# Two tiny activations moved, and the planner's costs corrected, in a one-core mixer layer

## The chip, the cores and the metric

The kernel runs on one core of a Trainium2 chip. The core has five engines with queues of their own: TensorE (PE) multiplies matrices into PSUM, VectorE (DVE) and ScalarE (ACT) work on elements, GpSimd (POOL) does the same more slowly and issues transfers that add to what lies at their target, and SyncE (SP) issues the plain transfers. Each engine runs its queue strictly in order, so an instruction that waits holds up everything behind it on that engine. ScalarE computes functions from tables; a function whose table is not the one in use needs an ACT_TABLE_LOAD in front of it.

The metric is the device time of one execution in microseconds, as the median over runs. A profiled execution gives the trace.

## The reference

One layer on x of 1024 tokens by 1024 channels, all in float32:

```python
c_act = jax.nn.silu(c)
mod = c_act @ mod_w[l] + mod_b[l]
shift, scale, gate = jnp.split(mod, 3, axis=-1)
h = rmsnorm(x, norm_g[l]) * (1.0 + scale[:, None, :]) + shift[:, None, :]
u = h @ w_in[l]                                   # 1024 -> 5 x 1024
cv, cg, cs, lx, ls = jnp.split(u, [...], axis=-1)

v = causal_depthwise_conv(cv * sigmoid(cg), dw_w[l], dw_b[l])      # 31 taps
v = silu(layernorm(v, cln_g[l], cln_b[l]))
y_conv = (v @ pw2_w[l] + pw2_b[l]) * silu(cs)

xs = causal_depthwise_conv(lx, sc_w[l], sc_b[l])                   # 4 taps
r, i = sigmoid(xs @ wr + br), sigmoid(xs @ wi + bi)                # 8 heads
log_a = -8 * r * softplus(-lam[l])
a = exp(log_a); mult = sqrt(-expm1(2 * log_a))
hs = linear_scan(a, mult * (i * xs))
y_lru = hs * silu(ls)

y = concatenate([y_conv, y_lru]) @ w_out[l]
out = rmsnorm(x + (1.0 + gate) * y, final_g)
```

## The kernel before

**Layout.** Channels lie on the 128 partitions, in KT = 8 tiles, and the 1024 tokens along the free axis, in two halves of 512. Every float32 operand of a large product is split into two parts, hi (rounded to the type that TensorE multiplies) and lo (the remainder), and a product is three matmuls: hi·hi, hi·lo and lo·hi. The hi of a weight is a cast on ScalarE (`whi`); its lo (`wlo`) comes by one of three ways, by the weight's number in the order: a subtraction on GpSimd (below EARLY = 20), a subtraction on VectorE (below LATE = 41), or a transfer. In the last way, `remainder` (L470), ScalarE writes the negated hi into `wlo` and GpSimd issues a transfer that adds the weight from HBM (for `ylc`, a tile) to it (`ADD`, L385). These transfers are the "DMA remainders": seven for the recurrent half of w_out (`wlo<-in_w_out_dram`), and some for the point-wise and last products (`wlopw`, `hlpw`, `wloout`, `hlout`, `ylc`).

**Stages.** (1) The start, to about 57 us: c goes through Silu and is spread over the partitions by TensorE, eight dot products on VectorE with mod_w give the scale, x is scaled into `uh` and `ul`, and the first four column tiles of w_in are multiplied (`first0` to `first3`, in PSUM). The RMS norm's divisor is only known once all of x has been squared: TensorE sums the squares (`token_stats`), ScalarE takes the root (L939, tile `st`), VectorE the reciprocal, and TensorE spreads it over the partitions, one half of the tokens at a time, from where ScalarE copies it to `rbc`. VectorE then multiplies the finished products by `rbc` (`first_u`). The second half of the fourth product has no PSUM buffer until then; it is computed afterwards, under the name `late`. (2) To about 472 us: the other 36 column tiles of w_in, eight pairs of gate products, with the convolutions, scans and the rest of the dot products on the other engines. (3) To about 565 us: the recurrent half of w_out, eight products of 48 matmuls (`ps<-yh,whi` and so on), and beside them the layer norm of the convolution: mean by TensorE, subtraction on VectorE and squares on ScalarE tile by tile (`lnss`, `lnsq`), sums by TensorE, root on ScalarE (`sd`), reciprocal, spread (`lnbc`), multiplication on VectorE, Silu on ScalarE. (4) To about 633 us the point-wise product (`xpw`, `ypw`, `zpw`), and (5) to the end the convolution's half of w_out (`xout`, `yout`, `zout`, `y`) with the final norm; both by a scheme of seven half-sized products in place of eight.

**How the order comes about.** Nothing in the program runs in the order in which it is written. Every operation is handed to a planner (class `Plan`) with an engine, a cost in microseconds, a priority (lower is sooner), and what it reads and writes. `Plan.order` plays a clock forward and, on each engine that is free, takes the ready operation with the lowest priority that finds its buffers free; the instructions are then emitted in the order of this play. So the planner's costs decide the order on the chip but not the time there. The costs that matter here:

- `SWITCH` (L131): what an activation costs more in the plan if its function's table is not in use. When choosing, 2.0 is added to the priority of such an operation. Abs, Square, copies and scalings have no table of their own in the plan.
- `LAND` (L93): how long after its issue a DMA remainder counts as landed, at the least.
- 0.18 us for each of the small matmuls that sum a block of 128 tokens (L727 in `rstd`, and L983).
- `LATENCY`: what passes until another engine, or the same, may use a result; 0.15 for ScalarE and VectorE.

An operation's result is not due before these times, and ScalarE, when it has nothing else that is ready, takes whatever is, whatever its priority.

**What the change touches.** The root of a constant at L753: an activation with Sqrt of one column, into `junk`, whose only use is that its table load stands early. `softplus8` (L1009): softplus of lam for eight values a partition, from Abs and Exp on ScalarE (tile `sp_u`) and a row of tiny VectorE operations. `layer_norm` (L1235). A second root of a constant stands ahead of the last product (L1441) and stays.

Of the kernel before, what the change touches and what calls it, by code (L numbers as in the profile page):

```python
# [11 lines left out]
AF = mybir.ActivationFunctionType  # L12
# [5 lines left out]
KT = D // P  # L18
# [71 lines left out]
GDOT = "DVE"  # L90
FOLD = "DVE"
EARLY = 20
LATE, LAND = 41, 4.5  # L93
ISSUE, FLIGHT, RATE = 1.0, 10.0, 3.0
GM = 17
TAPP = 25
# [29 lines left out]
class Plan:  # L126
# [1 line left out]


    LATENCY = {"SP": 2.0, "PE": 0.2, "ACT": 0.15, "DVE": 0.15, "POOL": 0.15}  # L130
    SWITCH = 1.3  # L131
    TICK, BUSY, COLD = 3.4133, 3060, 3.8

    def __init__(self, pools):
# [176 lines left out]
def hymba_layer(ctx: ExitStack, tc: tile.TileContext, xT, vecs, mod_w, w_first, w_in,  # L311
# [37 lines left out]
    def ACT(prio, out, in_, func, n=T, bias=None, scale=None, accum=None, r=(), w=(),  # L349
            reserve=0, after=()):  # L350
        kw = {}

        def emit():
            if func == "copy":
                act.copy(out(), in_())  # L355
                return
            if bias is not None:
                kw["bias"] = bias
            if scale is not None:
                kw["scale"] = scale  # L360
            if accum is not None:
                kw["accum_out"] = accum
            act.activation(out=out(), in_=in_(), func=func, **kw)  # L363
        ptr = sum(x is not None and not isinstance(x, float) for x in (bias, scale))
        return S.op("ACT", a_cost(n, ptr) + (0.1 if accum is not None else 0), emit, prio, r, w,
                    table=SETS.get(func), reserve=reserve, after=after)
# [48 lines left out]
    def halves(b, a, e):  # L415
        return [(b, i) for i in range(b.parts) if i * (T // b.parts) < e
                and a < (i + 1) * (T // b.parts)]
# [287 lines left out]
    def rstd(prio, sqs, a, e, ps, o, after=(), warm=(), idle=None):  # L705


        nb = (e - a) // P
        sd, rs = S.buf("sd", f"sd{prio}_{o}"), S.buf("rs", f"rs{prio}_{o}")
        wk = halves(ps, o, o + e - a)  # L710


        def warm_mm():
            pe.matmul(half(idle, 0)()[:, :P], ones, ones, start=True, stop=True)

        def stats(sq, k):
            for b in range(nb):
                pe.matmul(ps()[:, o + b:o + b + 1], sq()[:, a + b * P:a + b * P + P],
                          ones[:, 0:1], start=k == 0 and b == 0, stop=k == len(sqs) - 1,
                          skip_group_check=True)  # L720

        def spread(ps=ps):
            for b in range(nb):
                pe.matmul(ps()[:, o + b * P:o + b * P + P],
                          rs()[:, b:b + 1].to_broadcast([P, P]), ident, start=True, stop=True)
        for k, sq in enumerate(sqs):
            at = S.op("PE", 0.18 * nb, lambda sq=sq, k=k: stats(sq, k), prio, halves(sq, a, e), wk,  # L727
                      after=after if k == 0 else [])
            for _ in range(warm[k] if warm else 0):
                S.op("PE", 0.22, warm_mm, prio, [], [idle], after=[at], columns=4 * P)  # L730
        ACT(prio, lambda: sd()[:, :nb], lambda: ps()[:, o:o + nb], AF.Sqrt, nb, bias=eps_t,
            scale=1.0 / D, r=wk, w=[sd])
        S.op("DVE", 0.2, lambda: dve.reciprocal(rs()[:, :nb], sd()[:, :nb]), prio, [sd], [rs])
        op = S.op("PE", 0.22 * nb, spread, prio, [rs], wk, columns=4 * P * nb)
        if idle:
            S.op("PE", 0.22 * nb, lambda: spread(idle), prio, [rs], [idle], after=[op],
                 columns=4 * P * nb)
        return wk, op
# [11 lines left out]

    cs, ps_c = ctile("cs", KT), [mm_tile(f"c_row{z}") for z in (0, 1)]
    ACT(-130, lambda: cs, lambda: V[:, OFF["c"]:OFF["c"] + KT], AF.Silu, KT, w=[("cs", 0)])
    ACT(-101, lambda: junk, lambda: eps_t, AF.Sqrt, 1, r=[("cs", 0)], w=[("junk", 0)])  # L753

    def idle_mm():
        pe.matmul(psb()[:, :P], ones, ones, start=True, stop=True)
# [222 lines left out]
    def shift_mm():  # L979
        for i in range(len(FIRST + NEXT)):  # L980
            pe.matmul(psx()[:, i:i + 1], fsum()[:, i * P:i * P + P], ones[:, 0:1],
                      start=True, stop=True)
    S.op("PE", 0.18 * len(FIRST + NEXT), shift_mm, BIP, [fsum], [psx])  # L983
    ACT(BIP, lambda: bias, lambda: psx()[:, :len(FIRST + NEXT)], "copy", len(FIRST + NEXT), r=[psx],
        w=[("bias", 0)])

# [21 lines left out]

    def softplus8(pr, after):  # L1009
        lam = lambda: V[:, OFF["lam"]:OFF["lam"] + KT]  # L1010
        u, s, s2, q, r = (S.buf("sp_" + n, "sp_" + n) for n in ("u", "s", "s2", "q", "r"))
        ACT(pr, u, lam, AF.Abs, KT, w=[u])
        ACT(pr, u, u, AF.Exp, KT, scale=-1.0, r=[u], w=[u])
        TS(pr, s, u, 2.0, None, ALU.add, r=[u], w=[s], after=after)
        S.op("DVE", 0.2, lambda: dve.reciprocal(s(), s()), pr, [s], [s])
        TT(pr, "DVE", s, s, u, ALU.mult, KT, r=[s, u], w=[s])
        TT(pr, "DVE", s2, s, s, ALU.mult, KT, r=[s], w=[s2])
        TS(pr, q, s2, 1.0 / 17.0, 1.0 / 15.0, ALU.mult, ALU.add, r=[s2], w=[q])
        for n in (13, 11, 9, 7, 5, 3, 1):
            TT(pr, "DVE", q, q, s2, ALU.mult, KT, r=[q, s2], w=[q])  # L1020
            TS(pr, q, q, 1.0 / n, None, ALU.add, r=[q], w=[q])
        TT(pr, "DVE", q, q, s, ALU.mult, KT, r=[q, s], w=[q])
        TS(pr, r, lam, -1.0, 0.0, ALU.mult, ALU.max, w=[r])
        STT(pr, q, q, 2.0, r, ALU.mult, ALU.add, KT, r=[q, r], w=[q])
        TS(pr, lambda: sp8n, q, -8.0, None, ALU.mult, r=[q], w=[("sp8", 0)])
        TS(pr, lambda: sp8h, q, 4.0, None, ALU.mult, r=[q], w=[("sp8", 1)])
# [208 lines left out]
    def layer_norm():  # L1235
        pr = 45
        mean, hi, lo = mm_tile("mean"), big_buf("csh", F32R), big_buf("csl", F32R)
        split(-1, hi, lo, csum)
        for rhs, last in ((hi, False), (lo, True)):
            def mean_mm(rhs=rhs, last=last):  # L1240
                for a, b in FULL:
                    pe.matmul(mean()[:, a:b], ones_d, rhs()[:, a:b], start=not last, stop=last)
            S.op("PE", 2 * 0.2267, mean_mm, -1, [rhs], [mean], columns=2 * H)
        ss = big_buf("lnss")
        for t in range(KT):
            TT(pr, "DVE", c[t], c[t], mean, ALU.subtract, r=[c[t], mean], w=[c[t]])
            if t == 0:
                ACT(pr, ss, c[t], AF.Square, r=[c[t]], w=[ss])
            else:
                q = big_buf(f"lnsq{t}")  # L1250
                ACT(pr, q, c[t], AF.Square, r=[c[t]], w=[q])
                TT(pr, "DVE", ss, ss, q, ALU.add, r=[ss, q], w=[ss])
        bc = mm_tile("lnbc")
        rstd(-1, [ss], 0, T, bc, 0)
        for t in range(KT):
            TT(pr, "DVE", c[t], c[t], bc, ALU.mult, r=[c[t], bc], w=[c[t]])
            ACT(pr, c[t], c[t], AF.Silu, scale=vec("cln_g", t), bias=vec("cln_b", t), r=[c[t]],
                w=[c[t]])
# [266 lines left out]
```

## Time and profile before

| | |
|---|---|
| median of 3 runs | 733.63 us (732.92 to 734.35) |
| profiled execution | 734.38 us, of which the span from first to last instruction is 732.5 us |
| granted TensorE clock | 0.996 |
| TensorE / VectorE / ScalarE / GpSimd busy | 99% / 83% / 63% / 22% of the span |
| table loads on ScalarE | 45, 1.283 us each, 57.7 us in all |
| DMA remainders for the recurrent half | 7, 512 KB each, 6.3 to 9.8 us from the start of the issue to the landing |

A row of the order of time reads: start in us, length in us, engine, line, operation, what it writes <- what it reads, shapes, count, and in brackets the engine's idle time just before it and what ended it. Rows that follow one another on an engine may be merged into one with a count. A row of the list of waits reads: who waited, <- for whom, us in total, times, longest. A matmul's row is longer than the distance from one matmul's start to the next, since they overlap: 512 columns start every 0.227 us.

### The profile page before, as it was taken

How to read it: one execution, taken by the hardware profiler on the slowest of the kernel's cores; microseconds unless marked ns; L12 is line 12 of the kernel's file. 1: busy time of each engine (PE TensorE's matmuls, PEld its weight loads, DVE VectorE, ACT ScalarE, POOL GpSimd, SP SyncE). 2: the span in 40 equal slices, each digit the busy share in tenths (PEclk: the TensorE clock that was granted, in tenths of full speed). 3: DMA queues.
4: the chain of work that ended last, by engine and by line, in shares of the span. 5: the costliest groups of instructions: out<-in, count | busy, mean ns of one | idle time of the engine just before them, and what ended most of it. 6: DMA issues, size and time to landing. Idle time of an engine off the chain costs nothing.

```text
span 732.5 us, 8976 instructions
## 1 busy us (share of the span) xinstructions
PE 722.9 (99%) x3292; PEld 601.2 (82%) x3292; DVE 611.2 (83%) x832; ACT 459.4 (63%) x579; POOL 159.6 (22%) x147
## 2 busy tenths in 40 slices
PE   9999999999999999999999999999999999999996
PEld 8888888888888887888888888888888888878885
DVE  7999999989559996888598999839698566999647
ACT  7650677656669759956848789517594345755322
POOL 0024012344524222232215111320000001010003
PEclk9999999999999999999999999999999999999998
DMA  8961023358888999799753644686666846784006
GB/s 342 408 223 58 0 82 84 86 115 191 196 209 183 239 243 215 179 224 211 161 114 85 154 90 120 173 233 174 170 158 152 227 117 138 221 217 167 20 15 216
DMA packets 40508, 121.03 MB, mean 165 GB/s; under 512 B 4496, under 2 KB 13200, under 8 KB 40464
## 3 DMA queue, kind: packets, MB, share of 16 engines
q0 software_dynamic: 15552, 43.70, 33.0%
q1 hardware_dynamic: 23904, 75.84, 30.3%
q10 hardware_dynamic: 1008, 0.92, 0.4%
q8 instruction: 26, 0.43, 0.2%
q14 instruction: 18, 0.15, 0.1%
HBM read 72.55 MB, written 12.58 MB: 116 GB/s over the span
## 4 chain that ended last, share of the span: by engine, by line
PE 69%; DVE 13%; issue 11%; DMA 3%; ACT 3%; POOL 1%; DVEq 0%; POOLq 0%; ACTq 0%
PE ps L506 46%; PE xout L675 5%; PE xpw L675 5%; PE ypw L675 3%; DVE modw L374 2%; DVE caccs L374 2%; PE gate L1205 2%; PE y L650 2%; PE zpw L675 1%; DMA wloout<-in_w_out_dram 1%; DVE ul L374 1%; DVE cacc L374 1%; PE zout L675 1%; DMA oo<-co 1%; DMA wlo<-in_w_out_dram 1%
## 5 line engine op out<-in xcount | busy, mean ns | idle before, releaser
L506 PE MATMUL ps<-uh,whi 128*128 128x512 f32 x576 | 177.6, 390 | 0.3 <-ACT scs L363 0.3
L506 PE MATMUL ps<-ul,whi 128*128 128x512 f32 x576 | 177.4, 389 | 0.0
L506 PE MATMUL ps<-uh,wlo 128*128 128x512 f32 x576 | 177.3, 389 | 0.0
L506 PEld LDWEIGHTS ps<-uh,whi 128*128 128x128 f32 x576 | 107.9, 188 | 23.3 <-ACT scs L363 1.0
L506 PEld LDWEIGHTS ps<-ul,whi 128*128 128x128 f32 x576 | 108.1, 188 | 22.5
L506 PEld LDWEIGHTS ps<-uh,wlo 128*128 128x128 f32 x576 | 108.1, 188 | 22.5
L355 ACT CAST whi<-raw 128x1024 fp32r<-128x1024 f32 x44 | 45.9, 1047 | 69.9 <-PE ps L506 44.9
L387 POOL DMA_DIRECT2D es<-cq x45 | 41.1, 936 | 128.0 <-ACT cq L363 91.7
L382 POOL TENSOR_TENSOR wlo<-raw,whi 128x1024 fp32r<-128x1024 f32 x16 | 40.3, 2530 | 126.0 <-ACT whi L355 85.1
L363 ACT ACT_TABLE_LOAD x45 | 57.7, 1283 | 5.8 <-DMA oo<-co 4.3
L374 DVE SCALAR_TENSOR_TENSOR cacc<-v,V,cacc 128x511 f32<-128x511 f32 (+14 forms) x75 | 55.6, 742 | 0.5
L374 DVE SCALAR_TENSOR_TENSOR caccs<-v,V,caccs 128x511 f32<-128x511 f32 (+6 forms) x70 | 52.1, 744 | 2.3 <-ACT caccs L363 1.1
L374 DVE SCALAR_TENSOR_TENSOR caccs<-c,wsum,caccs 128x511 f32<-128x511 f32 (+6 forms) x70 | 52.0, 743 | 1.0
L387 POOL DMA_DIRECT2D oo<-co x42 | 37.9, 948 | 61.7 <-ACT co L363 25.3
L506 PE MATMUL ps<-yh,wlo 128*128 128x512 f32 x128 | 39.6, 391 | 0.2 <-DMA wlo<-in_w_out_dram 0.2
L506 PE MATMUL ps<-yh,whi 128*128 128x512 f32 x128 | 39.6, 391 | 0.0
L506 PE MATMUL ps<-yl,whi 128*128 128x512 f32 x128 | 39.5, 389 | 0.0
L382 DVE TENSOR_TENSOR wlo<-raw,whi 128x1024 fp32r<-128x1024 f32 x21 | 27.5, 1311 | 5.8 <-ACT whi L355 5.8
L363 ACT ACTIVATE cq<-v,V 128x511 f32<-128x511 f32 (+14 forms) x45 | 31.8, 706 | 0.1
L374 DVE SCALAR_TENSOR_TENSOR xs<-ps,V,xs 128x1023 f32<-128x1023 f32 (+2 forms) x24 | 30.6, 1273 | 0.0
L374 DVE SCALAR_TENSOR_TENSOR modw<-modw,sc 128x1024 f32<-128x1024 f32 x23 | 30.1, 1312 | 0.0
L363 ACT ACTIVATE cq<-c,wsum 128x512 f32<-128x512 f32 x42 | 29.6, 711 | 0.0
(334 smaller groups left out, 1458.1 us busy)
## 6 DMA issues: line engine op xcount, KB each, us to landing
raw<-in_w_in_dram SPq DMA_DIRECT2D x36, 512.0 KB, 4.5
modw<-in_mod_w_dram SPq DMA_DIRECT2D x24, 512.0 KB, 7.9
scsd<-scs SPq DMA_DIRECT2D x8, 512.0 KB, 4.3
raw<-in_w_out_dram SPq DMA_DIRECT2D x8, 512.0 KB, 4.1
accd<-acc SPq DMA_DIRECT2D x8, 512.0 KB, 4.5
rawpw<-in_pw_dram SPq DMA_DIRECT2D x8, 512.0 KB, 4.1
scsr<-scsd SPq DMA_DIRECT2D x8, 512.0 KB, 4.9
rawout<-in_w_out_dram SPq DMA_DIRECT2D x8, 512.0 KB, 3.3
```

What stands on the lines that cost most here:

```text
L355: act.copy(out(), in_())
L363: act.activation(out=out(), in_=in_(), func=func, **kw)
L374: dve.scalar_tensor_tensor(out=out(), in0=in0(), scalar=scalar, in1=in1(), op0=op0, op1=op1, accum_out=accum)
L382: lambda: e.tensor_tensor(out=out(), in0=a(), in1=b(), op=op), prio, r, w,
L387: return S.op("POOL", ISSUE, lambda: pool.dma_start(out(), a(), accum_op=ALU.add), prio, r, w, lag=RATE * n / T, after=after, flight=flight)
L506: pe.matmul(ps()[:, a - off:b - off], k3(lhs)()[:, k, :], rhs[k]()[:, a:b], start=(k == 0 and lhs is wh and rhs is xh and (a - off) % H == 0),
L650: pe.matmul(to(), half(*lhs)()[:, j * P:j * P + P], half(*rhs)()[:, c0:c1], start=a == "S1" and j == 0 and t == 0, stop=j == KT // 2 - 1 a ...
L675: pe.matmul(half(ps, 0)(), half(*lhs)()[:, j * P:j * P + P], half(*rhs)(), start=start and j == 0 and t == 0, stop=j == KT // 2 - 1 and t ...
L1205: pe.matmul(ps()[:, c0:c1], lhs()[:, j, :], rhs()[:, c0:c1], start=st == 0, stop=st == 2)
```

## The change

The Abs and Exp of `softplus8` leave that function and are given priorities −129 and −128, straight after the Silu of c; the root of a constant now waits for Exp's result and has priority −127 (before: −101, after the Silu of c). In the layer norm, another root of the constant is put after the first square, with priority −1. The planner's numbers become LAND 6.0, SWITCH 1.283 and 0.224 for the small sums.

```diff
-LATE, LAND = 41, 4.5
+LATE, LAND = 41, 6.0
...
-    SWITCH = 1.3
+    SWITCH = 1.283
...
-            at = S.op("PE", 0.18 * nb, lambda sq=sq, k=k: stats(sq, k), prio, halves(sq, a, e), wk,
+            at = S.op("PE", 0.224 * nb, lambda sq=sq, k=k: stats(sq, k), prio, halves(sq, a, e), wk,
...
     ACT(-130, lambda: cs, lambda: V[:, OFF["c"]:OFF["c"] + KT], AF.Silu, KT, w=[("cs", 0)])
-    ACT(-101, lambda: junk, lambda: eps_t, AF.Sqrt, 1, r=[("cs", 0)], w=[("junk", 0)])
+    sp_u = S.buf("sp_u", "sp_u")
+    ACT(-129, sp_u, lambda: V[:, OFF["lam"]:OFF["lam"] + KT], AF.Abs, KT, w=[sp_u])
+    ACT(-128, sp_u, sp_u, AF.Exp, KT, scale=-1.0, r=[sp_u, ("cs", 0)], w=[sp_u])
+    ACT(-127, lambda: junk, lambda: eps_t, AF.Sqrt, 1, r=[sp_u], w=[("junk", 0)])
...
-    S.op("PE", 0.18 * len(FIRST + NEXT), shift_mm, BIP, [fsum], [psx])
+    S.op("PE", 0.224 * len(FIRST + NEXT), shift_mm, BIP, [fsum], [psx])
...
-        u, s, s2, q, r = (S.buf("sp_" + n, "sp_" + n) for n in ("u", "s", "s2", "q", "r"))
-        ACT(pr, u, lam, AF.Abs, KT, w=[u])
-        ACT(pr, u, u, AF.Exp, KT, scale=-1.0, r=[u], w=[u])
+        u = sp_u
+        s, s2, q, r = (S.buf("sp_" + n, "sp_" + n) for n in ("s", "s2", "q", "r"))
...
-                ACT(pr, ss, c[t], AF.Square, r=[c[t]], w=[ss])
+                o = ACT(pr, ss, c[t], AF.Square, r=[c[t]], w=[ss])
+                ACT(-1, lambda: junk, lambda: eps_t, AF.Sqrt, 1, w=[("junk", 0)], after=[o])
```

## The prediction

> **What bounds the kernel now.** I read the busy shares first, then TensorE's own list of waits, then the order of time at the places where that list has an entry, because only there can a change shorten the run.
>
> ```profile
> PE 722.9 (99%) x3292; PEld 601.2 (82%) x3292; DVE 611.2 (83%) x832; ACT 459.4 (63%) x579; POOL 159.6 (22%) x147
> ...
> PE token_stats L756 <- DVE ones L432: 1.1, 1, 1.1
> PE finbc L724 <- DVE rs65.7_0_5731 L733: 0.9, 1, 0.9
> PE late L799 <- DVE first_u L382: 0.8, 1, 0.8
> PE xout L675 <- DMA wloout<-in_w_out_dram: 0.4, 1, 0.4
> PE ps L506 <- ACT scs L363: 0.3, 1, 0.3
> PE ps L506 <- DMA wlo<-in_w_out_dram: 0.2, 1, 0.2
> ```
>
> TensorE works through 99% of the span, and the change gives it the same 3292 matmuls. All its waits together are 3.7 us: 1.1 at the very start, 0.9 in the closing norm, and four in between of 0.8, 0.4, 0.3 and 0.2. So the gain has a floor: what the change does to ScalarE counts only as far as it reaches one of these waits or makes a new one.
>
> **The start: exponential before root.** ScalarE's first 6 us, and the place where the first root is needed for the result:
>
> ```profile
> 3.05 1.28 ACT L363 ACT_TABLE_LOAD   x1
> 4.34 0.20 ACT L363 ACTIVATE junk<-eps_t 128x1 f32<-128x1 f32 x1
> 4.57 1.28 ACT L363 ACT_TABLE_LOAD   x1
> 5.86 0.21 ACT L363 ACTIVATE sp_u<-sp_u 128x8 f32<-128x8 f32 x1
> 5.97 0.57 ACT L355 COPY sc<-c_row 128x512 f32<-128x512 f32 x1
> ...
> 43.20 1.28 ACT L363 ACT_TABLE_LOAD   x1
> 43.43 1.22 DVE L374 SCALAR_TENSOR_TENSOR modw<-modw,sc 128x1024 f32<-128x1024 f32 x1
> 44.50 0.27 ACT L363 ACTIVATE st<-token_stats,eps_t 128x8 f32<-128x8 f32 x1
> 46.56 1.05 PE L934 MATMUL token_stats<-ident,st 128*128 128x128 f32 x8
> 46.97 2.78 POOL L382 TENSOR_TENSOR wlo<-raw,whi 128x1024 fp32r<-128x1024 f32 x1 [45.66 <-ACT whi L355]
> 47.41 2.36 DVE L958 TENSOR_TENSOR shift<-macc,V 128x1 f32<-128x1 f32 x1
> 49.53 1.05 PE L934 MATMUL token_stats<-ident,st 128*128 128x128 f32 x8
> 50.62 0.59 ACT L355 COPY rbc<-token_stats 128x512 f32<-128x512 f32 x1 [0.49 <-PE token_stats L934]
> 50.62 1.87 DVE L382 TENSOR_TENSOR first_u<-first,rbc 128x512 f32<-128x512 f32 x3
> 51.35 0.50 PE L799 MATMUL late<-uh,fhi 128*128 128x512 f32 x1 [0.77 <-DVE first_u L382]
> ```
>
> Before, the planner had slipped the low-priority Abs and Exp into an idle moment after the root of a constant: the load for the root (3.05) was undone by the load for Exp (4.57), and the root had to be loaded again at 43.20. After, Exp follows Abs and the root comes last: still two loads and two tiny operations before the copy at 5.97 (2×1.28 + 0.20 + 0.21), so the start costs 0, and what covers it is unchanged, the vector c's matmuls and the first dot product. The third load, 1.28 at 43.20, falls away: no other load lies between the two places, so the copies, squares and scalings there run with whatever table is in, and the root's is still in when it is wanted.
>
> What is that worth? The root could end near 43.5 instead of 44.77. But VectorE starts a 1.22 row at 43.43; if the planner puts the reciprocal behind it, it runs near 44.7 and the gain is 0.1, otherwise about 1.2. TensorE is not waiting there either: the first spread stands at 46.56, 1.8 after the root, because the planner filled the time with matmuls. In the plan the root is 1.3 (the old SWITCH) cheaper, so the spreads move one or two groups of three matmuls (0.68 each) ahead, and with them both rbc copies. TensorE has the same work, so the only prize is the 0.77 in front of `late`. `late` needs a PSUM buffer, which it gets from first_u of the fourth product or from the second rbc copy; both end near 51.2 now. With the spreads 0.7 to 1.4 earlier the copy ends near 50, before TensorE has run out of the earlier products at 50.6: gain 0.77. If `late` instead gets the buffer of the fourth product, whose own matmuls then end last (50.6 instead of 49.5), the evacuation (1.87 / 3 = 0.62) plus the hand-overs on both sides gives an idle of about 1.0, so a loss of 0.25. Ends: −0.77 and +0.25. I take −0.77, since the planner's due time for `late` is the first free buffer and the copy is the one that moves.
>
> [...]
>
> **The layer norm: a root of a constant after the first square.**
>
> ```profile
> 494.34 1.06 ACT L363 ACTIVATE lnss<-c 128x1024 f32<-128x1024 f32 x1 [7.01 <-DVE c L382]
> 495.47 1.07 ACT L363 ACTIVATE lnsq<-c 128x1024 f32<-128x1024 f32 x1
> 496.44 1.03 ACT L355 CAST whi<-raw 128x1024 fp32r<-128x1024 f32 x1
> ...
> 499.79 0.86 POOL L387 DMA_DIRECT2D wlo<-in_w_out_dram  x1 [12.97 <-ACT wlo L363]
> ...
> DMA to landing us min/median/max: 7.0/7.0/7.0
> ...
> 507.39 0.61 PE L506 MATMUL ps<-yh,wlo 128*128 128x512 f32 x2
> ...
> 511.40 1.28 ACT L363 ACT_TABLE_LOAD   x1
> 515.17 0.27 ACT L363 ACTIVATE sd-1_0_4068<-lnbc,eps_t 128x8 f32<-128x8 f32 x1 [2.48 <-PE lnbc L718]
> 520.77 1.05 ACT L355 CAST whi<-raw 128x1024 fp32r<-128x1024 f32 x1 [5.33 <-PE ps L506]
> 521.84 1.28 ACT L363 ACT_TABLE_LOAD   x1
> 523.13 1.25 ACT L363 ACTIVATE c<-c,V 128x1024 f32<-128x1024 f32 x1
> 524.28 1.04 ACT L363 ACTIVATE wlo<-whi 128x1024 fp32r<-128x1024 f32 x1
> ...
> 525.73 0.88 POOL L387 DMA_DIRECT2D wlo<-in_w_out_dram  x1 [15.25 <-ACT wlo L363]
> ...
> 533.22 0.73 PE L506 MATMUL ps<-yh,wlo 128*128 128x512 f32 x2 [0.24 <-DMA wlo<-in_w_out_dram]
> ```
>
> On the chip this load is hidden already: it ran at 511.40, and the root then waited 2.48 more for TensorE's sums. Moving it gains 0 by itself. It moves 1.28 + 0.20 = 1.48 to about 495.4, and there a tight transfer is queued behind it on ScalarE: cast whi, negated copy wlo, GpSimd's accumulating transfer at 499.79, landing 7.0 later at 506.8, first used at 507.39, so 0.6 of slack. The preload's priority (−1, plus 2 for a change of table) beats everything ready. By the code's costs it is ready 1.25 after the first subtraction (0.15 + 0.95 + 0.15) and the second square 1.285 after it (1.135 + 0.15), so it goes before that square; the square then takes the gap between whi and wlo that another square filled before. So wlo is late by 1.48 − 0.97 = 0.5, within the slack: cost 0. If the second square goes first, wlo is late by 1.48 and TensorE idles 0.88. Ends 0 and +0.9; I take 0.
>
> Without the switch in its cost, and with the sums at 0.224 a block instead of 0.18 (8 × 0.044 = 0.35 longer), the planned root ends 0.95 earlier, so the spread moves up by no or one product group (1.36) and the first Silu with it. That Silu and its load would then start near 519.7 and hold the cast of 520.77 until 522.2, but only one Silu (1.25) instead of load and Silu (2.53) stands between cast and wlo: 1.4 lost, 1.3 won, 0. Ends: −0.4 (the stop before 533.22 is gone; from start to start it is 0.85 instead of 0.45) and +1.1 (cast held and nothing won).
>
> **LAND 4.5 to 6.0, SWITCH 1.283, sums 0.224.** None of these touches an instruction; they move due times. With 6.0 the transfer of 499.79 is due at 506.7, before its use at 507.39; that of 525.73 at 532.6, where it is needed. So later landings change hardly any choice: 0. The other transfers of this kind have more room, also the 0.4 at xout, whose transfer was late against either value. The tail's sums grow by 0.18 for four blocks, which may put one matmul more before a spread that has work beside it: 0, ends ±0.4.
>
> What I cannot see is the re-listing between 60 and 470 us: from the moved root on, every due time shifts, and the greedy planner breaks its near ties anew.
>
> ```profile
> 60.00:160.00 100.00, 100.00 (x450) 83.06 (x449) 96.28 (x161) 56.19 (x70) 22.64 (x17) 1.00 0.30 73
> ```
>
> Columns are the length, then busy time of TensorE, weight loads, VectorE, ScalarE and GpSimd. VectorE has 4% left in the first stretch while TensorE has none. I take 0; ends −0.3 (the scs wait goes) and +3.4 (below).
>
> **Sum:** −0.77 + 0 + 0 + 0 = −0.77. The profiled execution took 734.38 (span 732.5 and 1.9 around it), 0.75 above the median of 733.63; the sum gives 733.6 there and 732.9 against the median.
>
> **Rivals.**
> *All the small waits go* (faster). A plan with truer costs also clears the others: 0.77 + 0.4 + 0.3 + 0.2, with about 0.2 of slow restart at each of the last three (0.85 between two starts before 533.22 is 0.40 over the usual 0.45, 0.16 more than the wait shown), 2.3: 731.3. For it: each is under a microsecond late. Against: only `late` hangs on something the change removes.
> *A PSUM evacuation falls behind a table load* (slower). At 60 to 290 us ScalarE's order is new; the scs evacuation already held TensorE here:
>
> ```profile
> 276.96 1.28 ACT L363 ACT_TABLE_LOAD   x1
> ...
> 281.62 0.70 ACT L363 ACTIVATE cq<-v,V 128x499 f32<-128x499 f32 x1
> ...
> 286.59 1.01 ACT L363 ACTIVATE scs<-ps 128x1024 f32<-128x1024 f32 x1
> ```
>
> One load and one to three products more ahead of it are 1.28 + 0.7 to 2.1, 2.0 to 3.4 less the 0.77: 734.9 to 736.3. It decides as soon as one load slips in there, because the wait shows no slack. Against: ScalarE also has 1.28 less to do at 43 us.
> *The change does nothing at the root and the preload holds the weights*: +0.25 + 0.88 = 1.1, 734.8.
> [...] The mechanism in rows: the shift held VectorE until 49.77, just after GpSimd's row of 46.97 ended at 49.75, and first_u queued behind it, so the wait could stay at 0.8 whatever the root does, and the time at 733.6; that lies inside my forecast's class, of which I give it a third.
>
> **Chances.** A measurement of this kernel tells about 0.2% (1.5 us) from no change. Forecast and its neighbours within that, 0.38, with the third rival in it in part; all waits gone or a little more, faster by over 0.2%: 0.30; re-listing or preload costing over 1.5: 0.32. Range: from the first rival's 731.3 to the second's upper end 736.3 leaves out a tenth on each side, for a luckier plan and two evacuations late; the forecast's own range is 732.2 to 734.8.
>
> **What would show it.** Right: no table load between 7 us and the root at about 43.3; `late` without a wait; a load near 495.5 and none at 511; wlo issued near 500.3 and no TensorE wait at 507. Wrong: a wait of 1.0 at `late`, of 0.9 at 507, or new entries in TensorE's waits between 60 and 470 us; a count of table loads that changes by more than the one would mean that they were re-ordered elsewhere.

## The result, and the profile after

The changed kernel takes 735.13 us in the median (733.42 to 737.08), the kernel before, on the same chip, 733.17 (732.03 to 734.35). The ratio is 1.0029, with a 95% interval of 1.0018 to 1.0039: slower by 0.29%, 2.0 us. The prediction had said 732.9; the time lies inside its range, on the wrong side of no change.

The profiled execution of the changed kernel took 736.26 us, its span 734.5, against 734.38 and 732.5. This is its row of busy times and TensorE's list of waits:

```profile
PE 724.3 (99%) x3292; PEld 601.6 (82%) x3292; DVE 615.3 (84%) x832; ACT 459.0 (62%) x579; POOL 159.0 (22%) x147
...
PE gate L1207 <- DVE xsl L382: 1.4, 1, 1.4
PE token_stats L759 <- DVE ones L432: 1.1, 1, 1.1
PE finbc L724 <- DVE rs65.7_0_5732 L733: 0.9, 1, 0.9
PE lnbc L718 <- DVE lnss L382: 0.4, 1, 0.4
PE ps L506 <- ACT scs L363: 0.3, 1, 0.3
```

The waits at `late`, `xout` and `wlo` are gone, and two new ones have come: 1.4 in front of a product of the gates, for `xsl`, and 0.4 in front of the layer norm's sums. VectorE is busy for 4 us longer with the same 832 instructions; that row turned out to be the one that matters.

The start, in order of time, for the instructions that the prediction followed there:

```profile
3.06 1.28 ACT L363 ACT_TABLE_LOAD   x1
4.35 0.21 ACT L363 ACTIVATE sp_u<-sp_u 128x8 f32<-128x8 f32 x1
4.58 1.28 ACT L363 ACT_TABLE_LOAD   x1
...
42.40 0.25 ACT L363 ACTIVATE st<-token_stats,eps_t 128x8 f32<-128x8 f32 x1
...
46.00 1.29 DVE L382 TENSOR_TENSOR first_u<-first,rbc 128x512 f32<-128x512 f32 x2
...
46.99 5.23 POOL L382 TENSOR_TENSOR wlo<-raw,whi 128x1024 fp32r<-128x1024 f32 x2 [45.68 <-ACT whi L355]
47.20 2.74 DVE L374 SCALAR_TENSOR_TENSOR fsum<-fraw,shift,fsum 128x512 f32<-128x512 f32 x1
...
47.75 0.59 ACT L355 COPY rbc<-token_stats 128x512 f32<-128x512 f32 x1
...
49.54 0.39 PE L802 MATMUL late<-uh,fhi 128*128 128x512 f32 x1
```

As forecast there are two loads at the start and none before the root, the second `rbc` copy ends near 48.3 instead of 51.2 (0.9 of which is this trace's earlier start of the first product, see the table below), and `late` starts without a wait. The layer norm:

```profile
497.77 0.88 POOL L387 DMA_DIRECT2D wlo<-in_w_out_dram  x1 [7.88 <-ACT wlo L363]
...
500.26 1.28 ACT L363 ACT_TABLE_LOAD   x1
...
515.93 1.23 DVE L382 TENSOR_TENSOR lnss<-lnss,lnsq 128x1024 f32<-128x1024 f32 x1 [0.46 <-DVE lnss L382]
...
517.31 1.92 PE L718 MATMUL lnbc<-ones,lnss 128*128 128x1 f32 x16 [0.36 <-DVE lnss L382]
```

The early load stands behind the first square, as planned. But that square starts at 499.19, and in the kernel before it started at 494.34; the sums start 4.0 us later (517.31 against 513.29), and TensorE now waits for the last of them. So the transfer that the prediction had queued behind the load is issued ahead of it, at 497.77.

Where the time went is best seen by comparing the same matmul in two traces: TensorE runs nearly the same 3292 in both. The table gives start in this kernel minus start in the kernel before, at the matmul which the kernel before starts at the time in the heading; the difference at the first product, given apart, is taken off. Negative is ahead. The kernels named e1 to e16 are those of the next section.

| kernel | first product | at 91 us | 377 | 425 | 459 | 537 | end |
|---|---|---|---|---|---|---|---|
| changed | −0.90 | −1.07 | −0.80 | +1.24 | +1.54 | +3.32 | +2.83 |
| e3 | −0.60 | −1.07 | −0.72 | +1.27 | +1.61 | +1.80 | +1.19 |
| e4 | −0.87 | +0.23 | +0.42 | +2.42 | +2.81 | +2.65 | +2.56 |
| e5 | −0.49 | −1.08 | −1.86 | −1.86 | +0.47 | +0.94 | +1.18 |
| e6 | −1.07 | −1.07 | −0.84 | +3.84 | +3.84 | +3.21 | +2.56 |
| e7 | −0.58 | −1.09 | −1.18 | +2.23 | +2.23 | +1.51 | +1.58 |
| e9 | −0.69 | −1.07 | −1.62 | −1.62 | −0.97 | −1.19 | −1.82 |
| e11 | −1.00 | −1.07 | −0.95 | −0.95 | −0.95 | −1.30 | −1.10 |
| e13 | −0.34 | −1.07 | −1.85 | −1.85 | −1.85 | −1.92 | −2.57 |
| e14 | −0.59 | −1.07 | −1.20 | −0.58 | −0.58 | −1.00 | −0.79 |
| e15 | −0.49 | +0.10 | −0.68 | −0.68 | −0.68 | −1.21 | −1.85 |
| e16 | −0.86 | +0.07 | −0.62 | −0.62 | −0.62 | −1.17 | −1.04 |

The first column isn't the change's doing (last section). The row of the changed kernel reads: 1.07 won by 91 us, 2.0 lost between 377 and 425, 1.8 more between 459 and 537, at the layer norm, 1.7 of which is a stretch at half the clock (last section). The trace of e3, with the same list but for the early load, is without that stretch: it loses 0.2 there and ends at +1.19.

Each row is one execution, and rows of kernels with the same lists differ: e3, e5, e9 and e13 have the changed kernel's list on every engine up to 382 us, and stand between −0.72 and −1.86 at 377. More than half of that difference is the wait of 0.3 at `scs`, at 286 us, and the slow restart behind it (together, in the changed kernel, 1.30 us from 285.21 on for three matmuls that otherwise take 0.68), which some of these traces have and others don't. What a later move does is read from the columns behind it.

### The profile page after: what moved, and what is told of

Its sections match the earlier page's. It is cut to its first block, busy times and chain, and to the rows that moved or that the text cites. A ratio compares the mean times of both kernels' runs of the same rounds, so it can differ in the third digit from the quotient of the medians.

```text
span 734.5 us, 8968 instructions
## 1 busy us (share of the span) xinstructions
PE 724.3 (99%) x3292; PEld 601.6 (82%) x3292; DVE 615.3 (84%) x832; ACT 459.0 (62%) x579; POOL 159.0 (22%) x147
## 5 line engine op out<-in xcount | busy, mean ns | idle before, releaser
L363 ACT ACTIVATE co<-v,V 128x511 f32<-128x511 f32 (+13 forms) x42 | 29.3, 707 | 0.4 <-DMA es<-cq 0.4
```

## The experiments

The kernel before, run beside each group of them, took 733.0 to 733.3 in the median. e4, e6, e7, e14 and e15 are planned anew; the others take the planner's list of the kernel named and move in it only the operations shown. In e14 and e15, too, the move is made in the finished list.

### The parts of the change by themselves

**e1, the root behind Exp, all else in the order of the kernel before:**

```diff
+        ops.remove(self.root)
+        ops.insert(ops.index(self.exp) + 1, self.root)
```

> The order of the kernel before, untouched, except that the root of a constant is issued right after Exp (one table load fewer, at 43 us). Theory that only a wait of TensorE is worth anything: the load at 43.2 us is gone, the wait of 0.8 us at `late` goes or shrinks because the cast whi, and with it GpSimd's subtraction and the blocked shift, start about 1.3 us sooner; 0.0 to 0.8 us faster than before, 732.4 to 733.2. Rule that the whole load counts: 1.3 us faster, 731.9. Theory that the start itself is harmed: slower.

Measured 733.42, ratio 1.0001 (0.9992 to 1.0010). Its order of time at the root and at `late`:

```profile
42.57 0.25 ACT L366 ACTIVATE st<-token_stats,eps_t 128x8 f32<-128x8 f32 x1
...
45.02 3.43 POOL L385 TENSOR_TENSOR wlo<-raw,whi 128x1024 fp32r<-128x1024 f32 x1 [43.72 <-ACT whi L358]
...
46.13 2.88 DVE L377 SCALAR_TENSOR_TENSOR fsum<-fraw,shift,fsum 128x512 f32<-128x512 f32 x1
...
50.65 0.50 PE L802 MATMUL late<-uh,fhi 128*128 128x512 f32 x1 [0.76 <-DVE first_u L385]
```

The load of 1.28 us is gone and the root stands at 42.57 instead of 44.50 (0.65 of that is the trace's earlier start), and `late` waits 0.76 as ever, where I had expected the wait to go or shrink: the spreads stand where the list has them, and VectorE is held in `fsum` (2.88 for 0.75) while GpSimd's `wlo` runs. Taking the load away is worth nothing by itself; the wait goes only with the new list of the start, in which the spreads stand earlier (e11).

**e2, the root of a constant behind the layer norm's first square, all else in the order of the kernel before:**

```diff
+        late.bufs, late.emit = [], self.preload
+        ops.insert(ops.index(self.first) + 1, late)
```

> The order of the kernel before, untouched, with the root of a constant issued behind the first square of the layer norm. Theory of the re-ordering (the loss comes from the order between 370 and 450 us, the preload costs little): 0 to 0.9 us slower than before, 733.2 to 734.1, from the weight cast queued behind it. Theory that the preload itself is the loss: sums of the layer norm late by 1 us or more, TensorE waits for them and in some executions runs a stretch at half clock: 735 or more, with a wider spread of the runs.

Measured 733.85, 1.0005 (0.9994 to 1.0016). The load stands at 495.81, the next transfer of a weight is issued at 501.51 instead of 499.79, and TensorE has no wait at 507. The price that the prediction put at 0 is 0 as far as this can tell, but by luck: the transfer is 1.7 late and not 0.5, since the squares that follow keep their places ahead of it, and it lands 6.2 us after its issue where it had taken 7.0, at 507.7, 0.1 before its use at 507.80.

**e3, the changed kernel in its order, without the layer norm's constant root** (its result is used by nothing):

```diff
+        ops.remove(self.skip)
```

> The order of the changed kernel, untouched, but the root of a constant in the layer norm is not issued (its load then comes before the real root, at about 510 us). Theory of the re-ordering: the waits at the gate product near 412 us stay (1.4 us and what follows), 0 to 1 us better than the changed kernel, 734.1 to 735.1. Theory that the preload is the loss: about 2 us better than the changed kernel, 733.1, and no stretch at half clock near 520 us.

Measured 734.96, 1.0027 (1.0014 to 1.0039). Both new waits, 1.4 and 0.4, are there without the early load. It isn't the load that makes them.

**e4, the kernel before with one planner's cost changed:**

```diff
-    SWITCH = 1.3
+    SWITCH = 1.283
```

> The kernel before with only SWITCH = 1.283 in place of 1.3. Not one operation is added, removed or given another priority. Theory of the re-ordering: the gate product near 412 us waits for xsl as in the changed kernel, about 2.0 to 2.5 us slower than before, 735.2 to 735.7, since the gain at the start is missing. Theory that the preload or the start makes the loss: as before, 733.2.

Measured 735.19, 1.0025 (1.0016 to 1.0033), with 1.4 at the gate and 1.0 at `late`. No instruction is added or removed, 0.017 us in a cost that no engine sees, and the loss at the gates is there in full: +0.42 at 377 us, +2.42 at 425. 67 of VectorE's instructions stand at other places than before, and between 100 and 495 us the order on every engine is the changed kernel's. So the loss at the gates comes from the re-listing. LAND can be left out: the changed kernel planned with 4.5 in place of 6.0 gives every engine the same list. The 0.224 by itself was not measured.

**e6 and e7, the moves with the old costs** (e6 both moves, e7 the exponential's alone, each planned anew):

```diff
-LATE, LAND = 41, 6.0
+LATE, LAND = 41, 4.5
...
-    SWITCH = 1.283
+    SWITCH = 1.3
...
-            at = S.op("PE", 0.224 * nb, lambda sq=sq, k=k: stats(sq, k), prio, halves(sq, a, e), wk,
+            at = S.op("PE", 0.18 * nb, lambda sq=sq, k=k: stats(sq, k), prio, halves(sq, a, e), wk,
```

> Both moves of the change (Exp ahead of the root, root ahead of the layer norm's) with the planner's old numbers. Theory that SWITCH 1.283 alone brings the bad order: no wait at gate 6, the gain at the start of about 1 us stays; 732.3 to 733.3. Theory that any re-ordering from the moved root on is as bad: another wait of 1 us or more somewhere between 60 and 470 us, 734.5 or more.

> Only Exp ahead of the root of a constant, planned with the old numbers. If the start's gain is real and the layer norm's preload costs what it did with the old order (0 to 0.5 us): 732.2 to 733.0, `late` without a wait. If the gain at the start was only the clock's earlier rise in one execution: 733.3.

Measured 736.23 (1.0036; 1.0023 to 1.0049) and 737.0 (1.0051; 1.0034 to 1.0067), both with 1.9 of wait for `xsh` and 0.6 for `xsl` around gates 5 and 6. Keeping the old costs gives a third list, and it loses too; both of e7's expectations were missed. 1.7 of e6's +3.84 at 425 us is a stretch at half the clock, which e7's trace, with the same list up to 498 us, is without. Of e7's 3.7 us its trace, its fastest execution, shows only 1.6. Three of its six executions, its slowest, had a lower granted clock (0.991 to 0.994, last section); how much of the rest that is isn't known.

### Where the wait sits

**e5, both products of gate 6 two groups of matmuls later on TensorE**, in the changed kernel's list; **e8** is the same without the layer norm's constant root:

```diff
+        late = [self.g[6, 0], self.s[6, 0], self.g[6, 1]]
+        at = ops.index(self.g[6, 1])
+        at = next(k for k in range(at + 1, len(ops)) if ops[k].eng == "PE")
+        ops[at + 1:at + 1] = late
+        for o in late:
+            ops.remove(o)
```

> The changed kernel with one thing moved in its order: both products of gate 6 stand two groups of matmuls later on TensorE (2.7 us), every other engine's order as it was. Theory that the loss is TensorE reaching gate 6 before VectorE has made xsl: the wait of 1.4 us is gone and with it the slow restarts around it (2.0 us in the trace); 1.5 to 2.0 us faster than the changed kernel, 733.1 to 733.6, level with the kernel before. Theory that VectorE is simply behind by then and the wait comes back at the next use: 735.

> The changed kernel with gate 6 two groups later and the layer norm's root of a constant not issued. Theory: the start's 1.0 us is left as gain, the wait for the layer norm's sums (0.4 us) and the chance of a stretch at half clock stay, as the order there is the changed one; 732.4 to 733.3. Theory that the preload delays those sums: the wait is gone too, 0.5 us or more under the run with the preload.

Measured 735.37 (1.0032; 1.0020 to 1.0044) and 735.42 (1.0029; 1.0016 to 1.0043). My theory, that gate 6 merely stood too early on TensorE, fell: its wait is gone and stands at gate 7 instead, larger. From the list of waits of e5:

```profile
PE gate L1215 <- DVE xsl L390: 2.0, 1, 2.0
```

VectorE was late as a whole, and whoever asked next paid.

**e9, e5 with gate 7's operand ahead of gate 6's scan on VectorE:**

```diff
+        for o in (self.l[7], self.xr[6], self.h[7]):
+            ops.remove(o)
+            ops.insert(ops.index(self.tap[7]) + 1, o)
```

> The changed kernel with gate 6's products two matmul groups later on TensorE, as before, and gate 7's operand earlier on VectorE: the last tap of xs7, its cast xsh and its remainder xsl go ahead of gate 6's scan (2.28), copy step (0.72) and sls product (1.22). Theory (re-listing left VectorE's remainders for gates 6 and 7 too late, and nothing else is lost there): the 2.0 us wait of TensorE at gate 7's xsl goes, and the kernel takes 733.4, which is 735.4 less 2.0. Rival (VectorE is behind as a whole between 400 and 460 us): a wait of about 2 us stands at the next thing that TensorE or ScalarE needs of VectorE, the scan or the sls product, and the time stays 735.4.

Measured 732.28, 0.9990 (0.9981 to 0.9998). The wait at gate 7 is gone, with 0.4 left for an evacuation behind it, and the lead of the start reaches the end (table). Better by 1.1 than expected: the layer norm's wait of 0.4 went as well; the rest isn't accounted for.

**e10, e9 with the layer norm's sums one group later:**

```diff
+        k = ops.index(self.ln_sums)
+        at = next(j for j in range(k + 1, len(ops)) if ops[j].eng == "PE")
+        ops.insert(k, ops.pop(at))
```

> As the run just before, and the layer norm's sums one matmul group (1.4 us) later on TensorE. Theory (the two gate waits and the wait of 0.4 to 0.5 at the sums are all that the new order loses): 732.9, no wait above 0.5 between 60 and 640 us. Rival (the sums' lateness is passed on to the root and the spread that follow): 733.4, with a wait of TensorE at the spread in place of that at the sums.

Measured 733.82, 1.0009 (0.9998 to 1.0021). The rival held and more: TensorE waits 0.6 at the spread, and 0.7 for a late `wloout` near 655 us. These two don't make up the 1.5 by which it is above e9 in the median; two of its eleven executions also had a lower granted clock (0.994, last section).

**e11, the start in the changed kernel's order, the rest, from 109 us of the plan, in that of the kernel before; e12, the same with e2's early load:**

```diff
+        first = [self.ops[k] for k in HEAD]
+        seen = set(HEAD)
+        ops = first + [o for o in ops if o.seq not in seen]
```

> The kernel before with its own order from 109 us of the plan on; ahead of that its operations stand in the changed kernel's order, the Softplus exponential ahead of the root among them. No root ahead of the layer norm's. Theory (the start's new order is worth the 1.0 us wait at late, and the loss comes from the new order of 370 to 530 us alone): 732.2, with before's small waits at 507 us and 654 us. Rival (TensorE runs into what VectorE and ScalarE deliver at gates 5 to 7 at their own pace, whatever the order): 733.3, with new waits of about 1 us in all at the gates between 380 and 440 us.

> As the run just before, and the root of a constant behind the first square of the layer norm, the rest in the order of the kernel before. Theory (the early load is hidden and costs nothing; the wait at wlo was TensorE's only loss at 507 us): 732.2 to 731.7, without the load behind the sums. Rival (the 1.48 us on ScalarE cost 0.5, which the earlier run of this move alone, 733.85, leaves open): 732.7.

Measured 732.17 (0.9987; 0.9978 to 0.9996) and 732.4 (0.9988; 0.9979 to 0.9997). e11 is 0.84 below the 733.01 of the kernel before beside it, and the prediction had summed 0.77: the start's prize is real, and the middle in its old order keeps it. Against e11 the changed kernel's new list from 109 us on costs 2.8 in the medians (−0.84 against +1.96). The traces place 2.0 of that at the gates and 0.2 at the layer norm; the rest they don't place, apart from the clock. e12 lies between its two expectations, 0.2 from e11 and inside the intervals. VectorE's last part of gate 6's operand and the product that needs it, first in e11, then in the changed kernel, then in the kernel before:

```profile
411.45 1.22 DVE L414 TENSOR_TENSOR xsl<-xs,xsh 128x1024 fp32r<-128x1024 f32 x1
...
414.14 0.62 PE L1237 MATMUL gate<-xsl,ghi 128*128 128x512 f32 x2
```

```profile
413.64 1.20 DVE L382 TENSOR_TENSOR xsl<-xs,xsh 128x1024 fp32r<-128x1024 f32 x1
...
414.89 0.74 PE L1207 MATMUL gate<-xsl,ghi 128*128 128x512 f32 x2 [1.44 <-DVE xsl L382]
```

```profile
413.40 1.22 DVE L382 TENSOR_TENSOR xsl<-xs,xsh 128x1024 fp32r<-128x1024 f32 x1
...
416.09 0.62 PE L1205 MATMUL gate<-xsl,ghi 128*128 128x512 f32 x2
```

In e11 VectorE is ahead of the kernel before by as much as TensorE is (1.95, of which 1.00 is the trace's earlier start). In the changed kernel TensorE is ahead and VectorE isn't: 413.64 against 413.40. What is left is why.

### Why VectorE is late

Going back from 413 us on VectorE in the changed kernel, the first rows that are longer than their like stand at 383 to 392 us, and GpSimd's rows beside them are the sums of the convolution's channels for the layer norm (`csum`). The order of time there, in the changed kernel:

```profile
382.48 2.41 POOL L382 TENSOR_TENSOR csum<-c,c 128x1024 f32<-128x1024 f32 x1 [8.66 <-issue]
383.45 2.52 DVE L382 TENSOR_TENSOR yl<-sls,yh 128x1024 fp32r<-128x1024 f32 x1
384.96 3.28 POOL L382 TENSOR_TENSOR csum<-csum,c 128x1024 f32<-128x1024 f32 x1
...
386.54 2.78 DVE L382 TENSOR_TENSOR xsl<-xs,xsh 128x1024 fp32r<-128x1024 f32 x1
388.79 2.80 POOL L382 TENSOR_TENSOR csum<-csum,c 128x1024 f32<-128x1024 f32 x1
389.25 3.42 DVE L382 TENSOR_TENSOR wlo<-raw,whi 128x1024 fp32r<-128x1024 f32 x1
```

and in the kernel before:

```profile
384.18 2.41 POOL L382 TENSOR_TENSOR csum<-c,c 128x1024 f32<-128x1024 f32 x1 [11.81 <-DVE c L382]
386.44 1.24 DVE L382 TENSOR_TENSOR xsl<-xs,xsh 128x1024 fp32r<-128x1024 f32 x1
387.15 6.13 POOL L382 TENSOR_TENSOR csum<-csum,c 128x1024 f32<-128x1024 f32 x2
389.26 1.75 DVE L382 TENSOR_TENSOR wlo<-raw,whi 128x1024 fp32r<-128x1024 f32 x1 [1.59 <-ACT whi L355]
```

The same three sums and, but for `yl`, the same remainders. Before, a transfer's issue lay between the first sum and the second, and `xsl` ran in that gap (1.24); only `wlo` met a sum (1.75), with 1.59 of idle time ahead of it. After, `yl` has moved in beside the first sum and the transfer behind the second, and the rows take 2.52, 2.78 and 3.42. Against the 1.22 that each takes alone that is 5.1 us, against before's 0.5, and no idle time is left until gate 6. The rows show how: each of the three ends 1.08 us after the sum that was running when it started (384.89, 388.24 and 391.59), whenever it started itself, and so does before's `wlo` (391.01 against 389.93). A row that adds into PSUM, `caccs`, runs beside the second sum from 385.90 and takes its usual 0.73.

The planner counts such collisions: in `Plan.order`, `lock` and `held` make GpSimd's operations and those of VectorE that read two tiles, none of them in PSUM, wait for each other. But it counts them by its own times. In its play `yl` starts ahead of the first sum, and VectorE loses to the sums once, at `xsl`; on the chip the first sum started 0.97 ahead of `yl`, and VectorE lost three times.

The theory: these collisions make VectorE late. The rival: the order of its own rows does. The next four kernels move GpSimd's three sums alone, to 440 us and later, and leave every other engine's list as it is; they differ in the kernel that they start from.

```diff
+        names = [{b.name for b in o.bufs} for o in ops]
+        at = ops[names.index({"es5", "cq5_14"})]
+        for o in self.sums[2::-1]:
+            ops.remove(o)
+            ops.insert(ops.index(at) + 1, o)
```

**e13, from the changed kernel:**

> The changed kernel with GpSimd's first three channel sums (csum) moved from 382 us to behind the transfer es of gate 7's stretch at 442, where VectorE stands idle for 3.4 and 5.8 us; the order on every other engine is the changed kernel's. Theory A (in the new order these sums fall on VectorE's remainders yl, xsl and wlo, which take 2.52, 2.78 and 3.42 there in place of 1.2 to 1.75; VectorE is then 4 us late and has no idle time to catch up before gate 6): the three rows take 1.2 to 1.3 each, the wait of 1.4 at gate 6's xsl is gone, TensorE keeps its lead of 1 us past 460 us, and the kernel takes 733.1. Theory B (the order of VectorE's own rows and the earlier place of gate 6 on TensorE make the wait): the wait stays at 1.0 or more and the time at 735.1.

Measured 731.45, 0.9981 (0.9972 to 0.9991). Its order of time and its whole list of TensorE's waits:

```profile
382.96 1.21 DVE L389 TENSOR_TENSOR yl<-sls,yh 128x1024 fp32r<-128x1024 f32 x1
...
384.74 1.22 DVE L389 TENSOR_TENSOR xsl<-xs,xsh 128x1024 fp32r<-128x1024 f32 x1
...
387.08 1.23 DVE L389 TENSOR_TENSOR wlo<-raw,whi 128x1024 fp32r<-128x1024 f32 x1 [1.12 <-ACT whi L362]
...
409.43 1.21 DVE L389 TENSOR_TENSOR xsl<-xs,xsh 128x1024 fp32r<-128x1024 f32 x1
...
412.54 0.62 PE L1214 MATMUL gate<-xsl,ghi 128*128 128x512 f32 x2
...
440.52 2.73 POOL L389 TENSOR_TENSOR csum<-c,c 128x1024 f32<-128x1024 f32 x1
443.32 5.74 POOL L389 TENSOR_TENSOR csum<-csum,c 128x1024 f32<-128x1024 f32 x2
```

```profile
PE token_stats L766 <- DVE ones L439: 1.1, 1, 1.1
PE finbc L731 <- DVE rs65.7_0_5732 L740: 0.9, 1, 0.9
PE first L809 <- DVE uh L403: 0.8, 1, 0.8
```

The three remainders take 1.2, gate 6's `xsl` comes at 409.43 instead of 413.64, and no wait is left between the first products and the final norm. The time is 3.7 below the changed kernel's and 1.7 below what the theory had asked for. The layer norm's wait went, too. The wait at `scs` is also gone, but it stood at 286 us, ahead of the moved sums, and e5's trace lacks it as well, so this is a difference between executions. From 377 us on, where the move can act, this trace gains 0.7 and that of e3 loses 1.9.

**e14, from e7; e15, from e4; e16, the control, from the kernel before:**

> The kernel with the exponential ahead of the root alone and the old costs, which took 737.0, with the same three sums moved in the same way. There the sums stand at 372 to 381 us, and VectorE's c<-v and wlo take 2.24 and 3.88. Theory A: both rows come back to 1.2 or less, the waits of 1.9 at gate 5 and 0.6 at gate 6 go, and the time falls by 2.5 or more, to 734.5 or less. Theory B: both waits stay within 0.5 of what they were, 737.0.

> The kernel before with SWITCH 1.283 alone, which took 735.2, with the same three sums moved in the same way. Theory A: wait of 1.4 at gate 6 gone, the wait of 1.0 at late stays, 733.2. Theory B: 735.2.

> Control: the kernel before with the same three sums moved in the same way. There the sums at 384 to 393 us meet VectorE only in one wlo (1.75 for 1.2), with 2.5 us of idle time behind it, so under theory A as under B nothing changes: 733.3, with no new wait at the gates. If the move by itself is worth 1 us or more here, it says nothing about the collision in the other three runs.

Measured 732.59 (0.9995; 0.9986 to 1.0004), 732.97 (0.9995; 0.9986 to 1.0003) and 733.23 (1.0000; 0.9991 to 1.0010). In e14 the collisions of its own list, 2.24 and 3.88, are back at 0.69 and 1.22, both gate waits are gone, and 4.4 us with them. In e15 the gate's wait is gone and that at `late`, 0.9, stays; 2.2 us. Moving the sums in the kernel where they hurt nobody, e16, gives nothing: it stands at −0.62 at 377, 425 and 459 us. At their new place there they stretch two rows of VectorE to 2.69 and 3.42, and TensorE waits for neither, so a collision by itself is no loss. In the three lists that lose and were tried, the cause is shown by taking it away: no other engine's list differs. GpSimd's transfers behind the sums also come sooner, but VectorE waited for none of them: in the changed kernel it had no idle time from 383.45 to 413.64.

The runs show that much: the remainders take 2.52, 2.78 and 3.42 beside `csum`, and 1.21 to 1.23 without it. What in the chip holds the row was not shown.

## Why the prediction was right or wrong

**The start: right in mechanism and in size, incomplete in its condition.** The sum had −0.77 for the wait at `late`, from spreads that the planner moves ahead. The table has −1.07 by 91 us, and e11 −0.84 in the median. What the prediction left unsaid, e1 shows: without the new list of the start the missing load is worth 0. The last of the rivals, that GpSimd's hold on VectorE and not the root keeps `late` waiting, fits e1, where `fsum` is held (2.88 for 0.75); but the second copy of `rbc` comes no sooner there either, so e1 doesn't separate the two. In the changed kernel two of the three `first_u` get ahead of that row (46.00 against 47.20), and the copy comes sooner, and so the prize was paid.

**The layer norm's load: right in its price, not in its working.** Priced at 0 with the load hidden and `wlo` 0.5 late, inside a slack of 0.6; e2 and e12 have no wait at 507, and the load makes no difference beyond the intervals, there or in e3. But in e2 `wlo` was issued 1.7 late and a faster landing saved it by 0.1, which is luck, and in the changed kernel the transfer went ahead of the load.

**LAND: right.** No engine's list in the changed kernel depends on it.

**The re-listing: the step that failed.** "… every due time shifts, and the greedy planner breaks its near ties anew … I take 0; ends −0.3 … and +3.4." It was worth +2.0 at gates 5 to 7 in the traces, and 2.8 in all in the medians. The ends held it, and the prediction gave 0.32 to a re-listing or a preload that costs over 1.5; but the term was put at 0 without a reason. The kernel before is a list in which VectorE's remainders happen to miss all but one of GpSimd's sums. The new lists tried here (the changed kernel's, e4's and that of e6 and e7) do not miss them, and with TensorE at 99% and VectorE without idle time ahead of the gates each lost; that a re-listing costs more often than it wins is a guess from these.

**The slower rival had the wrong place.** It put 2.0 to 3.4 less the start's gain on an evacuation behind a table load on ScalarE, near 287 us. No load slipped in there, and the table loads are 44 where 45 were, the one less that was forecast. That its 734.9 to 736.3 holds the measured 735.13 is luck; the mechanism was VectorE's, at 383 us. The prediction looked at a long VectorE row beside a GpSimd row (2.36 at 47.41 beside 46.97) for `late` only. The same look at every place where a GpSimd row and a VectorE remainder stand near each other would have pointed at 384 to 391 us, where the kernel before escapes by one transfer's issue (0.87, at 386.54).

**What would show it** did its work: "new entries in TensorE's waits between 60 and 470 us" was on the list of what would be wrong, and that is the entry at 414.

## What to carry to other kernels

Where a planner orders the work, a change of its costs or of one early operation is a new list, and the new list is the change: measure the moves in the old order (e1, e2, e11) and the new order without the moves (e4) before crediting either. When an engine is late at a wait, walk back along its own rows to the first ones that are longer than their like; the cause may stand 30 us earlier and on a third engine, and curing it there (e13) is worth more than shifting the waiter (e5). The kernel to keep is e13, 731.45 against 733.17.

## What the runs showed of the hardware that was not expected

**TensorE's clock comes up at different times.** The first product starts between 7.48 and 8.56 us after the span's start over the 18 traces. In 16 of them it goes with the time at which the granted clock reaches full speed, 4.52 to 7.08 us: 7.08 in the kernel before and 4.96 in the changed kernel, whose lead in its trace holds 0.9 from that (the sixteen small matmuls of `c_row`, which start at 3.08 in both, take 3.76 there and 2.92 here). In e9 and e13, where full speed comes early (4.63 and 4.38), the first product waits 0.3 and 0.8 for `uh` instead. In a comparison of two traces this difference has to be taken off. It needs no change of the start: e16, whose start is the list of the kernel before, has −0.86 in the table. What sets the time of the turn was not shown.

**Half the clock for 3.4 us, in a kernel whose TensorE is busy for 99% of the span.** In the trace of the changed kernel the clock fell around the layer norm's spread. Stretches of the trace, with length, busy time of TensorE, weight loads, VectorE, ScalarE and GpSimd, and the granted clock behind them:

```profile
518.83:522.24 3.41, 3.41 (x18) 3.10 (x18) 1.49 (x2) 2.18 (x3) 0.00 (x0) 0.73 0.00 0
522.24:525.66 3.42, 3.42 (x18) 3.12 (x18) 1.50 (x2) 1.72 (x3) 0.87 (x1) 0.77 0.97 298
```

0.73 and 0.77 together are half speed for some 3.4 us, from 520.37 to 523.78 (between 521 and 523 us the granted clock is 0.50), and 1.7 us lost: in the table the changed kernel stands at +3.32 at 537 us where e3, with the same wait ahead of the sums, stands at +1.80. It follows a stop of 0.4 and sixteen sums of one column each. The trace of e6 has such a stretch too, from 390.42 to 393.83, behind its stops of 1.9 and 0.6. Between where full speed begins and the drop lie 515.41 us in the changed kernel's trace and 385.71 in e6's. In steps of the stretch's own length, 3.41 us in both traces, these are 151 and 113, of 3.413 us each (515.41 / 151, 385.71 / 113). That the clock keeps such steps is the author's estimate from these figures. Counted in them, the one just ahead of the drop holds the stop and the sums whole in the changed kernel's trace (516.95 to 520.37), and most of both stops in e6's. In the traces of e3, e5, e8 and e7, which have the same stops and no drop there, an edge of the steps cuts the sequence in two (at 517.60, 517.88, 518.59 and 388.11). The estimate fits six traces; no run was made to test it.

It isn't a chance that strikes all kernels alike. Executions with a mean granted clock of 0.994 or less are 2 of 13 of the changed kernel, 3 of 12 of e3, 1 of 6 of e5, 2 of 5 of e6, 3 of 6 of e7, 3 of 10 of e8 and 2 of 11 of e10; in e3, e5, e7 and e8 they are the slowest. The other kernels have none, nor have the 118 executions of the kernel before that were run beside them. All seven have, in their traces, either a wait at the layer norm or the 1.9 at gate 5, and the others have neither. So the lower clock is a part of what the new lists cost; whether the stops or the small sums bring it on stays open.
